# 32-byte gaps between split weights and two groups of split activations in an MLA/GLA decoder trunk

## The chip, the cores and the metric

The kernel runs on one core of a Trainium2 chip. The metric is the device time in microseconds of one execution. Before the change it is 1057.14 us, the median of three runs (1056.98 to 1057.34).

TensorE multiplies: it holds a stationary operand of 128 x 128 and streams a moving operand of up to 512 columns through it; sums collect in PSUM. In the profile a product is a MATMUL on PE with its LDWEIGHTS on PEld. VectorE is DVE, ScalarE is ACT, GpSimd is POOL, and SyncE (SP) starts most transfers. The operands of products lie in SBUF, where a tile takes the same bytes in each of 128 partitions; "at 32 modulo 128" says where in a partition it starts.

## The reference

Two layers, each a mixer and an MLP, all in float32 over a residual stream x of 512 tokens x 1024:

```python
for i in range(DEPTH):                       # 2
    xn = rms_norm(x, norm_mix[i])
    if i % 2 == 0:
        mix = mla_mixer(xn, ...)             # 8 heads, low-rank q and kv, rotary part, causal softmax
    else:
        mix = gla_mixer(xn, ...)             # 4 heads, gated linear attention, gate of rank 16
    x = x + mix
    xn = rms_norm(x, norm_mlp[i])
    x = x + jnp.square(jax.nn.relu(xn @ w_up[i])) @ w_down[i]   # 1024 -> 4096 -> 1024
return rms_norm(x, final_norm)
```

## The kernel before

**Split operands.** A float32 operand is kept as two tiles of the type float32r: `hi`, a rounded copy made on ACT, and `lo`, the rest, made on DVE (`split`, lines 102 to 107). A product is then three products, hi·hi, hi·lo and lo·hi, all into the same PSUM bank (`mm3`, lines 109 to 114). So nearly every product stands in a long row of products of the same shape, each with its own stationary operand.

**Where the operands live.** Four kinds of tile hold most operands:

- `wh` and `wl` hold split weights: three buffers each, filled by `piece` from the raw tiles `wraw` (loaded by SP) or, in the MLPs, `comb`.
- `set_A` holds both parts of one tile of split activations: 8 buffers of 4096 bytes, handed out by `both_parts`. The normalised input X of every mixer and MLP is here (`Norm.scaled`), as are V of the first mixer and the last weights of the second MLP.
- `set_B` holds one part each: 16 buffers of 2048 bytes, handed out by `slot("B")`. The hidden values of the MLPs, the latent values of the first mixer and the heads' outputs are here.
- Pools of their own hold the rest: `cq` and `ckv` (latent q and kv of the first mixer), `T1` to `T4` (combined inputs of the MLP), the tiles of both attentions. The profile leaves numbers out, so it shows both groups as `set` and T1 to T4 as `T`.

The allocator lays tiles out one after another, in the order in which their tags are first asked for, on multiples of 32 bytes. The order of first use is: constants, x, `wraw`, `wh`, `wl`, `set_A`, `set_B`, temporaries (`tmp`, `acc`, `rstd`), small statistics with `rtok`, then the pools that are opened and closed per stage.

**The stages.** The first mixer starts from weights loaded in five parts, each split and followed by the split of the x tiles it meets (the loop at the program's end that fills `w0`). Its input projection (line 408 and lines 112 to 114) has X moving under wh or wl; the projection to V has wh or wl moving and latent tiles stationary; the projections from the latent tiles have cq moving under weights, or weights moving over cq (the rotary part of q); then attention by heads and an output projection with the heads' outputs moving.

Each MLP (`mlp`) works through the 4096 hidden values in blocks of 512, seven of them with a scheme of seven smaller products in place of eight. Its up products (`up_product`, line 939) are 256 columns wide: weights stationary, X (set_A) or T1 to T4 moving, in runs of 24. Its down products (`down_product`, line 948) are 512 wide: hidden values (set_B) stationary, weights moving, in runs of 12. The two kinds alternate. The last block of the first MLP goes through line 1133 (weights stationary, hidden values in set_B moving), that of the second through line 1168 (hidden values stationary, weights split into set_A moving).

The second mixer (`gla`) has input projections of both forms: `proj_qk` with X moving, `b_type` with X stationary and weights moving.

A scheduler orders the instructions of each engine; data dependences and a few written-out orders (`keep_in_program_order`, `issue_after`) bind it.

Of the kernel before, what the change touches and what calls it, by code (L numbers as in the profile page):

```python
# [10 lines left out]
F32 = mybir.dt.float32  # L11
# [7 lines left out]
P = 128  # L19
D = 1024  # L20
S = 512
NT = S // P
# [28 lines left out]
def trunk_kernel(ctx: ExitStack, tc: tile.TileContext, t_in: dict, out: bass.AP):  # L51
# [4 lines left out]
    sb = ctx.enter_context(tc.tile_pool(name="sb", bufs=1))  # L56
    count = [0]

    def uname(s):
        count[0] += 1  # L60
        return f"{s}_{count[0]}"
# [40 lines left out]
    def split(src, hi, lo, hi_eng=ACT, lo_eng=DVE, order=lambda i: i):  # L102
        if hi_eng is ACT:
            order(ACT.activation(hi, src, AF.Copy))  # L104
        else:
            hi_eng.tensor_copy(hi, src)
        lo_eng.tensor_tensor(lo, src, f(hi), ALU.subtract)  # L107
# [29 lines left out]
    def piece(raw, a, n, order=lambda i: i):  # L137
        hi = sb.tile([P, a, n], F32R, tag="wh", bufs=3, name=uname("wh"))
        lo = sb.tile([P, a, n], F32R, tag="wl", bufs=3, name=uname("wl"))
        split(raw, hi, lo, order=order)  # L140
        return hi, lo
# [1055 lines left out]
    def gla(layer, nrm, vtag, ytag):  # L1197
# [82 lines left out]

        own = tmp((P, NT, P))
        DVE.tensor_tensor(own, nrm.rstd.rearrange("p (t c) -> p t c", t=NT), ident.unsqueeze(1).to_broadcast([P, NT, P]), ALU.mult)
        rtok = sb.tile([P, NT], F32, tag="rtok", name="rtok")
        DVE.reduce_sum(rtok, own, AX.X)


# [363 lines left out]
    warm = bank("a")  # L1650
    for _ in range(9):
        PE.matmul(warm[:, :P], ones128, ones128, start=True, stop=True)
    w0 = []
    for k0, k1 in ((0, 1), (1, 2), (2, 4), (4, 6), (6, 8)):
        w = piece(raw0[:, k0:k1], k1 - k0, KL, tc.keep_in_program_order)
        w0 += [(w, i) for i in range(k1 - k0)]
        for j in range(k0, k1):
            nrm.scaled(j, xT[j], tc.keep_in_program_order)
    mla_pools = []
    for name in ("mla_keep", "mla_pre"):  # L1660
        pool_es = ExitStack()
# [25 lines left out]
    mlp(0, n_mlp0, n_mix1)  # L1687
    psum_layout(False)
    Y, begun = gla(0, n_mix1, "B", "B")
    n_mlp1 = Norm(ND, inv_dr, "mlp", ND)  # L1690
    out_proj(t_in["gla_w_o"][0], Y, n_mlp1, begun)
# [23 lines left out]
def build(nc, shapes):  # L1715
    args = {}
    for name, (shape, dt) in shapes.items():
        args[name] = nc.dram_tensor(f"in_{name}_dram", shape, dt, kind="ExternalInput").ap()
    o = nc.dram_tensor("out_0_dram", (S, D), F32, kind="ExternalOutput").ap()
    with tile.TileContext(nc) as tc:  # L1720
        trunk_kernel(tc, args, o)
# [22 lines left out]
```

## Time and profile before

| | |
|---|---|
| median of 3 runs | 1057.14 us |
| profiled execution, its own time | 1057.37 us |
| span, first to last instruction | 1055.6 us |
| mean granted TensorE clock | 0.999 |
| PE busy | 1045.5 us, 99% of the span |
| PEld busy | 913.7 us, 87% |
| DVE busy | 876.0 us, 83% |
| ACT busy | 698.6 us, 66% |
| POOL busy | 113.4 us, 11% |
| mean DMA rate over the span | 142 GB/s |

A row of the groups reads: line, engine, operation, output<-inputs, the array's shape, the output's or moving operand's shape, xcount | busy us in total, mean ns of one | idle time of the engine just before, and what ended it. "ps<-T,wh" is a product into PSUM whose inputs are a T tile and a wh tile. A row of the chain reads: start in us, length in us, engine, output, line, and how many in a row. A row of the timeline reads: start, length, engine, line, operation, operands, shape, count.

### The profile page before, as it was taken

The page shows a single profiled execution, that of the slowest core. Times are in us where ns is not written, and L with a number is a line of the kernel's source. Part 1 is how long each engine was busy: PE and PEld are TensorE (multiplying, and loading weights), DVE is VectorE, ACT ScalarE, POOL GpSimd, SP SyncE. Part 2 cuts the span into 40 slices and gives each one's busy share as a digit, 9 for nine tenths or more (in the row PEclk, how much of TensorE's full clock was granted, in tenths as well). Part 3 has the DMA queues.
Part 4 walks back from the last instruction along what each step waited for, and adds up shares of the span by engine and source line. Part 5 has one row for each costly group of instructions (what it writes and reads, how often), then busy time and mean ns, then how long its engine had stood idle before and what let it go on. Part 6 is the DMA issues. An engine that isn't in the chain of part 4 may idle for free.

```text
span 1055.6 us, 15598 instructions
## 1 busy us (share of the span) xinstructions
PE 1045.5 (99%) x5966; PEld 913.7 (87%) x5966; DVE 876.0 (83%) x1340; ACT 698.6 (66%) x1074; POOL 113.4 (11%) x128
## 2 busy tenths in 40 slices
PE   9999999999999999999999999999999999999997
PEld 7888888889999999998888888878889999999985
DVE  7899977979889889898686498469889989989993
ACT  7667664577777767766445565655667777777784
POOL 7410011201101111000000000000011010010000
PEclk9999999999999999999999999999999999999999
DMA  7311235866966976842322221444496696696622
GB/s 231 90 51 41 81 79 160 238 176 150 235 181 150 229 192 146 221 147 93 90 80 80 80 80 51 126 105 132 110 248 132 178 254 140 176 249 152 165 81 80
DMA packets 120493, 149.97 MB, mean 142 GB/s; under 512 B 9345, under 2 KB 86145, under 8 KB 120289
## 3 DMA queue, kind: packets, MB, share of 16 engines
q1 hardware_dynamic: 95920, 117.76, 34.4%
q0 software_dynamic: 22400, 29.36, 17.4%
q10 hardware_dynamic: 2096, 1.84, 0.6%
q8 instruction: 47, 0.77, 0.3%
q14 instruction: 30, 0.24, 0.1%
HBM read 144.49 MB, written 4.19 MB: 141 GB/s over the span
## 4 chain that ended last, share of the span: by engine, by line
PE 95%; ACT 2%; DVE 2%; issue 0%; DMA 0%; ACTq 0%; SPq 0%; DVEq 0%
PE ps L939 26%; PE ps L948 25%; PE ps L112 10%; PE ps L114 10%; PE ps L113 10%; PE ps L1133 2%; PE ps L1388 2%; PE ps L129 1%; PE ps L1168 1%; PE ps L408 1%; PE ps L1515 1%; DVE wl L107 0%; PE ps L671 0%; PE ps L1438 0%; PE ps L667 0%
## 5 line engine op out<-in xcount | busy, mean ns | idle before, releaser
L948 PE MATMUL ps<-wh,set 128*128 128x512 f32 x784 | 258.5, 390 | 0.0
L107 DVE TENSOR_TENSOR wl<-wraw,wh 128x1024 fp32r<-128x1024 f32 x139 | 169.4, 1221 | 39.7 <-ACT wh L104 39.4
L104 ACT ACTIVATE wh<-wraw 128x1024 fp32r<-128x1024 f32 x139 | 145.9, 1053 | 82.1 <-PE ps L113 38.3
L948 PEld LDWEIGHTS ps<-wh,set 128*128 128x128 f32 x784 | 147.3, 188 | 28.8
L104 ACT ACTIVATE wh<-comb 128x1024 fp32r<-128x1024 f32 x112 | 118.8, 1061 | 62.8 <-PE ps L939 41.9
L939 PE MATMUL ps<-T,wh 128*128 128x256 f32 x896 | 159.8, 279 | 0.0
L948 PE MATMUL ps<-wl,set 128*128 128x512 f32 x392 | 153.7, 392 | 0.0
L107 DVE TENSOR_TENSOR wl<-comb,wh 128x1024 fp32r<-128x1024 f32 x112 | 136.7, 1220 | 18.6 <-ACT wh L104 16.9
L939 PEld LDWEIGHTS ps<-T,wh 128*128 128x128 f32 x896 | 140.5, 188 | 4.5
L939 PE MATMUL ps<-T,wl 128*128 128x256 f32 x448 | 125.1, 279 | 1.0 <-DVE wl L107 1.0
L939 PE MATMUL ps<-set,wh 128*128 128x256 f32 x672 | 122.6, 283 | 0.0
L939 PEld LDWEIGHTS ps<-set,wh 128*128 128x128 f32 x672 | 107.4, 191 | 3.2
L112 PE MATMUL ps<-set,wh 128*128 128x512 f32 x280 | 109.3, 392 | 0.7 <-ACT set L1557 0.3
L113 PE MATMUL ps<-set,wh 128*128 128x512 f32 x280 | 109.4, 391 | 0.0
L114 PE MATMUL ps<-set,wl 128*128 128x512 f32 x280 | 109.0, 390 | 0.0
L939 PE MATMUL ps<-set,wl 128*128 128x256 f32 x336 | 95.2, 283 | 0.0
L939 PEld LDWEIGHTS ps<-T,wl 128*128 128x128 f32 x448 | 84.2, 188 | 1.5 <-DVE wl L107 1.4
L948 PEld LDWEIGHTS ps<-wl,set 128*128 128x128 f32 x392 | 73.8, 188 | 11.6
L928 POOL DMA_DIRECT2D comb<-in_mlp_w_down_dram x28 | 33.6, 1201 | 421.0 <-DMA comb<-in_mlp_w_down_dram 155.5
L939 PEld LDWEIGHTS ps<-set,wl 128*128 128x128 f32 x336 | 64.3, 191 | 0.0
L112 PEld LDWEIGHTS ps<-set,wh 128*128 128x128 f32 x280 | 52.5, 188 | 12.6 <-ACT wh L104 1.0
L114 PEld LDWEIGHTS ps<-set,wl 128*128 128x128 f32 x280 | 52.6, 188 | 11.2 <-DVE wl L107 0.4
(396 smaller groups left out, 2024.2 us busy)
## 6 DMA issues: line engine op xcount, KB each, us to landing
comb<-in_mlp_w_down_dram SPq DMA_DIRECT2D x74, 512.0 KB, 5.0
wraw<-in_mlp_w_up_dram SPq DMA_DIRECT2D x32, 1024.0 KB, 5.8
comb<-in_mlp_w_down_dram POOLq DMA_DIRECT2D x28, 512.0 KB, 7.7
wraw<-in_gla_w_in_dram SPq DMA_DIRECT2D x12, 1024.0 KB, 5.3
comb<-in_mlp_w_up_dram SPq DMA_DIRECT2D x14, 512.0 KB, 3.8
comb<-in_mlp_w_up_dram POOLq DMA_DIRECT2D x14, 512.0 KB, 8.4
wraw<-in_mlp_w_up_dram POOLq DMA_DIRECT2D x14, 512.0 KB, 7.2
wraw<-in_mla_w_o_dram SPq DMA_DIRECT2D x4, 1024.0 KB, 5.0
```

What stands on the lines that cost most here:

```text
L104: order(ACT.activation(hi, src, AF.Copy))
L107: lo_eng.tensor_tensor(lo, src, f(hi), ALU.subtract)
L112: PE.matmul(psum, wh, xh, start=start, stop=False)
L113: PE.matmul(psum, wh, xl, start=False, stop=False)
L114: PE.matmul(psum, wl, xh, start=False, stop=stop)
L129: PE.transpose(psum, src, ident[: src.shape[0], : src.shape[0]])
L408: PE.matmul(p, w[:, i, j * P : (j + 1) * P], x, start=start, stop=stop)
L928: POOL.dma_start(t, q(b, *more), accum_op=ALU.add)
L939: PE.matmul(o, a_, x_, start=start and j == 0 and k == 0 and n == 0, stop=k == KH - 1 and n == 2, skip_group_check=True)
L948: PE.matmul(o, x_, w_, start=start and k == 0 and n == 0, stop=k == 1 and n == 2, skip_group_check=True)
L1133: PE.matmul(p, a, x, start=False, stop=k == 3 and n == 2, skip_group_check=True)
L1388: PE.matmul(p[:, t - t0], k[:, t * P : (t + 1) * P], moving[:, t], start=True, stop=True)
```

## The change

Two tiles of 8 float32 values (32 bytes) that nobody reads or writes are asked for at two places: `gap_a` after the first split of weights, and so behind wh and wl and ahead of set_A; `gap_b` after the first x tiles, and so behind set_A and ahead of set_B. And `rtok`, 16 bytes of use in a slot of 32, is asked for with 64 bytes more.

```diff
@@ in gla @@
-        rtok = sb.tile([P, NT], F32, tag="rtok", name="rtok")
+        rtok = sb.tile([P, NT + 16], F32, tag="rtok", name="rtok")[:, :NT]
         DVE.reduce_sum(rtok, own, AX.X)
@@ at the program's end @@
+    def gap(name, n):
+        sb.tile([P, n], F32, tag=name, bufs=1, name=name)
+
     w0 = []
     for k0, k1 in ((0, 1), (1, 2), (2, 4), (4, 6), (6, 8)):
         w = piece(raw0[:, k0:k1], k1 - k0, KL, tc.keep_in_program_order)
+        if k0 == 0:
+            gap("gap_a", 8)
         w0 += [(w, i) for i in range(k1 - k0)]
         for j in range(k0, k1):
             nrm.scaled(j, xT[j], tc.keep_in_program_order)
+    gap("gap_b", 8)
```

In the two built programs the order of instructions and their waits are the same on every engine. The tiles start here (bytes in a partition, and modulo 128):

| tile | before | after |
|---|---|---|
| wraw, first buffer | 36384, 32 | 36384, 32 |
| wh, first buffer | 52768, 32 | 52768, 32 |
| wl, first buffer | 65056, 32 | 65056, 32 |
| set_A, first buffer | 77344, 32 | 77376, 64 |
| set_B, first buffer | 110112, 32 | 110176, 96 |
| tmp, first buffer | 142880, 32 | 142944, 96 |
| rtok | 163616, 32 | 163680, 96 |
| cq, first | 168576, 0 | 168704, 0 |
| ckv, first | 180928, 64 | 181056, 64 |
| T1 to T4, comb | 64 | 64 |

All buffers of a kind have the same place modulo 128, since their sizes are multiples of 128, and so have the pieces of 128, 256 or 512 values that the products take from them. Behind rtok everything lies 128 bytes farther: 32 and 32 of the gaps, 64 of rtok.

## The prediction

> **What bounds the kernel now.** I read the page's first, second and fourth part, then the groups of instructions with shapes kept apart, then the chain that ended last, and last the timeline of TensorE product by product.
>
> ```profile
> PE 1045.5 (99%) x5966; PEld 913.7 (87%) x5966; DVE 876.0 (83%) x1340; ACT 698.6 (66%) x1074; POOL 113.4 (11%) x128
> ...
> PEclk9999999999999999999999999999999999999999
> ...
> PE 95%; ACT 2%; DVE 2%; issue 0%; DMA 0%; ACTq 0%; SPq 0%; DVEq 0%
> ```
>
> TensorE is busy for 99% of the span at the full granted clock, and 95% of the chain that ended last is its products. So what changes the step from one product to the next goes into the time almost in full, and the other engines have room. [...] Steps are read from start to start, or from the chain, which merges a run of products.
>
> ```profile
> L948 PE MATMUL ps<-wh,set 128*128 128x512 f32 x784 | 258.5, 390 | 0.0
> L939 PE MATMUL ps<-T,wh 128*128 128x256 f32 x896 | 159.8, 279 | 0.0
> L948 PE MATMUL ps<-wl,set 128*128 128x512 f32 x392 | 153.7, 392 | 0.0
> L939 PE MATMUL ps<-T,wl 128*128 128x256 f32 x448 | 125.1, 279 | 1.0 <-DVE wl L107 1.0
> L939 PE MATMUL ps<-set,wh 128*128 128x256 f32 x672 | 122.6, 283 | 0.0
> L939 PE MATMUL ps<-set,wl 128*128 128x256 f32 x336 | 95.2, 283 | 0.0
> ```
>
> L939 (the MLP's up products, 256 columns wide) does the same arithmetic with two kinds of moving tile. With T tiles one product's record is 279 ns, with set tiles 283 ns. Both load their weights from wh or wl. What tells the two apart is the place: wh and wl start at 32 modulo 128 bytes, T at 64, set at 32. The chain shows what that is worth as a step:
>
> ```profile
> 301.46 2.80 PE ps L939 x24
> 304.26 2.75 PE ps L948 x12
> 307.00 2.87 PE ps L939 x24
> 309.88 2.75 PE ps L948 x12
> 312.62 2.80 PE ps L939 x24
> ```
>
> The run at 307.00 has set tiles, those at 301.46 and 312.62 T tiles: 2.87/24 = 119.6 ns a step against 2.80/24 = 116.7 ns. No engine's idle time lies in these runs. So the place of operands does move TensorE's step, and apart operands are quicker here, by 2.9 ns.
>
> While a product streams its moving operand, the stationary operand of the next one is loaded:
>
> ```profile
> 54.22 0.39 PE L114 MATMUL ps<-set,cq2l 128*128 128x512 f32 x1
> ...
> 54.23 0.19 PEld L112 LDWEIGHTS ps<-wh,cq0h 128*128 128x128 f32 x1
> ```
>
> The load begins with the product before it (54.23 beside 54.22). The pair that can meet is therefore this product's moving tile and the next one's stationary tile. I call "distance" the second's start minus the first's, modulo 128 bytes. Now the 512-wide products, of which three runs in the first attention layer have different distances:
>
> ```profile
> 40.54 0.39 PE L112 MATMUL ps<-wh,set 128*128 128x512 f32 x1
> ...
> 43.48 0.39 PE L113 MATMUL ps<-wl,set 128*128 128x512 f32 x1
> ...
> 50.48 0.39 PE L113 MATMUL ps<-wl,cq0h 128*128 128x512 f32 x1
> ...
> 57.97 0.40 PE L112 MATMUL ps<-set,cq2h 128*128 128x512 f32 x1
> ...
> 62.84 0.39 PE L113 MATMUL ps<-cq0l,wh 128*128 128x512 f32 x1
> ...
> 64.71 0.39 PE L112 MATMUL ps<-ckv0h,wh 128*128 128x512 f32 x1
> ...
> 65.88 0.39 PE L114 MATMUL ps<-ckv1h,wl 128*128 128x512 f32 x1
> ```
>
> From 40.54 to 43.48 stand 13 steps at distance 0 (wh 32, set 32): 2.94/13 = 226 ns. From 50.48 to 57.97 stand 32 steps at distance 96 (wh or set at 32, cq at 0): 7.49/32 = 234 ns. From 62.84 to 64.71 stand 8 steps at distance 32 (cq 0, wh 32): 1.87/8 = 233.8 ns. From 64.71 to 65.88 stand 5 steps at distance 96 (ckv 64, wh 32): 1.17/5 = 234 ns. So for 512-wide products the sign is the other way round: equal operands give the short step, apart ones cost 6 to 8 ns more.
>
> A long run of equal ones outside this layer gives the value that most of the kernel has:
>
> ```profile
> 481.66 10.92 PE ps L1133 x48
> ```
>
> 10.92/48 = 227.5 ns; the down products above, 2.75/12 = 229.2 ns, since each run of 12 begins out of step after a 256-wide run.
>
> **The change part by part.** It adds no instruction and moves none: on all five engines the order and the waits of the two programs are the same. It moves set_A tiles (32 to 64 modulo 128), set_B tiles and the temporaries behind them (32 to 96); wh and wl stay at 32, and all that lies behind rtok moves by 128 bytes, so T, cq, ckv and the attention tiles keep their place. I counted in the program, product by product, how distances change; four groups matter.
>
> 1. *256-wide, distance 0 to 96*: 970 of them, the set products of L939, 42 runs of 24. Afterwards set_A is at 64 and wh at 32, which is just what T has now. Each run goes from 2.87 to 2.80 us: 42 x 0.07 = -2.9 us.
> 2. *512-wide, 0 to 96*: 531, set_A moving (64) under wh or wl (32): the input projections of both mixers and the MLPs' first block. The same two places as ckv under wh: 234 ns. From 227.5: 531 x 6.5 = +3.5 us. Another ckv run of that layer reads:
>
> ```profile
> 60.77 0.39 PE L112 MATMUL ps<-ckv0h,wh 128*128 128x512 f32 x1
> ...
> 61.93 0.40 PE L114 MATMUL ps<-ckv1h,wl 128*128 128x512 f32 x1
> ```
>
>    5 steps in 1.16 us, 232 ns. I take 233: +2.9 us, with 2.4 and 3.5 as ends.
> 3. *512-wide, 0 to 32*: 452, weights moving (32) with set_A stationary (64), and the last layer's output products. At 233.8 ns for 227.5: +2.8 us. The pair has not these very places in the trace, only their distance.
> 4. *512-wide, 0 to 64*: 1602, the largest group: 1077 of the 1176 products of L948 (wh or wl at 32 moving, set_B at 96 stationary), and 525 others, mostly the output projections with set_B moving. No steady 512-wide run at this distance is in the trace. Bounds: the slowest row, 234 ns, gives 1077 x 4.8 + 525 x 6.5 = +8.6 us; a gain like the 256-wide one, 2.9 ns each, gives -4.6 us. I take 233, near the first end, because both neighbours on either side of 0 (32 and 96) are slow at this width, and 64 lies farther from 0 than either: 1077 x 3.8 + 525 x 5.5 = +7.0 us.
>
> Everything else costs nothing by its rows. Vector and scalar engine also read and write at the moved places, but theirs does not depend on it:
>
> ```profile
> L107 DVE TENSOR_TENSOR wl<-wraw,wh 128x1024 fp32r<-128x1024 f32 x139 | 169.4, 1221 | 39.7 <-ACT wh L104 39.4
> L104 ACT ACTIVATE wh<-wraw 128x1024 fp32r<-128x1024 f32 x139 | 145.9, 1053 | 82.1 <-PE ps L113 38.3
> L104 ACT ACTIVATE wh<-comb 128x1024 fp32r<-128x1024 f32 x112 | 118.8, 1061 | 62.8 <-PE ps L939 41.9
> L107 DVE TENSOR_TENSOR wl<-comb,wh 128x1024 fp32r<-128x1024 f32 x112 | 136.7, 1220 | 18.6 <-ACT wh L104 16.9
> ```
>
> wraw is at 32, comb at 64, wh and wl at 32: 1221 against 1220 ns on DVE, 1053 against 1061 on ACT. Even 8 ns on each of ACT's thousand instructions would be 8 us of an engine that is idle a third of the time; what hides it is ACT's own slack (82.1 us before one of these groups), and TensorE's step, which grows. The few transposes and attention products that change distance (some 60 of 512 columns, a few 256- and 384-wide) may win or lose 0.3 us together.
>
> Sum: -2.9 + 2.9 + 2.8 + 7.0 = +9.8 us. The profiled execution took 1057.4 us (span 1055.6), 0.2 above the median of 1057.14, which is well inside what I claim. Forecast 1067.2 us.
>
> [...]
>
> **The rivals.**
> - *Distance 64 behaves as 0 at width 512.* It would if what repeats had a period of 64 bytes. Then group 4 is 0 and the time 1057.4 + 2.8 = 1060.2 us. Against it: 32 and 96 are alike at width 512, but no row tells 64 from 0 there.
> - *Distance 64 gains at width 512*, as 96 does at 256: 1057.4 + 2.8 - 4.6 = 1055.6 us.
> - *The other side: the 234 ns belong to the attention layer, not to distance.* There TensorE works beside many short ACT and DVE instructions. If those stretch its steps, groups 2 to 4 are 0 and only the gain of group 1 is left: 1054.5 us; if the wide products then gain 2.9 ns as well (2585 x 2.9 = 7.5), 1047.0. It decides where 512-wide products of the input projections, which have long equal runs now, show a step of 227 or less afterwards. Against it: the run at 40.54 lies in the same layer, 10 us earlier, and holds 226 ns.
> - *Nothing happens*, because what I read as distance is something else that T and cq tiles share: 1057.4 us. The places I used for group 1 are the very ones that T has now, which speaks against it.
>
> **How the numbers follow.** Forecast as summed, with group 4 slow: 0.58, 1063.5 to 1071. Distance 64 as 0: 0.20, about 1060. Distance 64 gains: 0.08. The attention layer's rows mislead: 0.10. Nothing: 0.04. The predicted time is 1067.2. The range leaves out the fourth case and the top of the first: 1055.5 (group 4 at its lower end) to 1070.5 (group 4 at 234 ns gives 1068.8, and 1.7 for runs of 12 that never come into step). A change of 0.2%, 2.1 us, is about the least that a measurement of this kernel can tell. Slower by more: 0.58 + 0.20 less a little = 0.77. Faster by more: the fourth case, 0.11 with a little of the third. Within: 0.12.
>
> **What would show it.** Right: L939 runs of 24 with set tiles at 2.80 us and their records at 279 to 280 ns; L948 runs of 12 at about 2.80 instead of 2.75 us; steps of 233 in the output projection (L1133, 11.2 us for 48); PE's busy time up by about 10 us with no new wait. Wrong: L948 at or under 2.75 us (then distance 64 is not slow), or the input projections still at 227 (then the attention layer's rows misled me), or a stall of TensorE that ends with ACT or DVE.

## The result, and the profile after

The changed kernel takes 1066.4 us (median of 3 runs, 1066.1 to 1066.66) against 1057.14 us before: a ratio of 1.0087, 95% interval 1.0064 to 1.011. The forecast was 1067.2 us. The span of the profiled execution grows from 1055.6 to 1064.6 us.

The page of the changed kernel, first, second and fourth part:

```profile
PE 1055.0 (99%) x5966; PEld 913.0 (86%) x5966; DVE 876.8 (82%) x1340; ACT 698.8 (66%) x1074; POOL 112.5 (11%) x128
...
PEclk9999999999999999999999999999999999999999
...
PE 97%; DVE 1%; ACT 1%; issue 0%; DVEq 0%
```

TensorE is busy 9.5 us longer over the same 5966 products, at the same granted clock (0.999); the busy times of the other engines move by less than 1 us. So the loss is in the steps of products. The groups of products, shapes kept apart (line, tiles, shape, count, then busy time and mean ns of one):

```profile
L948 PE MATMUL ps<-wh,set 128*128 128x512 f32 x784 | 262.1, 395 | 0.0
L939 PE MATMUL ps<-T,wh 128*128 128x256 f32 x896 | 161.4, 281 | 0.0
L948 PE MATMUL ps<-wl,set 128*128 128x512 f32 x392 | 154.6, 394 | 0.0
L939 PE MATMUL ps<-T,wl 128*128 128x256 f32 x448 | 125.9, 281 | 1.2 <-DVE wl L107 1.2
L939 PE MATMUL ps<-set,wh 128*128 128x256 f32 x672 | 119.9, 280 | 0.0
L939 PE MATMUL ps<-set,wl 128*128 128x256 f32 x336 | 94.0, 280 | 0.0
```

Against before, the down products (L948) go from 390 and 392 to 395 and 394 ns, the up products with set tiles (L939) from 283 to 280. The T rows go from 279 to 281 ns, and the prediction had left those alone. The chain that ended last, in the first MLP, says the same in steps:

```profile
303.23 2.85 PE ps L939 x24
306.08 2.80 PE ps L948 x12
308.88 2.81 PE ps L939 x24
311.68 2.79 PE ps L948 x12
314.47 2.82 PE ps L939 x24
...
484.71 11.00 PE ps L1133 x48
```

Runs of 12 down products take 2.79 to 2.80 us, where they took 2.75. Of the runs of 24, those with set tiles are at about 2.81 (2.87 before), and those with T tiles (303.23 and 314.47) take 2.85 and 2.82 (2.80 before). The output projection of the last block (L1133) takes 11.00 us instead of 10.92. And the projection to V that stood at 226 ns a step at 40.54 before (weights moving, set_B stationary), on the timeline:

```profile
40.17 0.39 PE L113 MATMUL ps<-wl,set 128*128 128x512 f32 x1
...
43.66 0.40 PE L113 MATMUL ps<-wl,set 128*128 128x512 f32 x1
```

15 steps in 3.49 us, 232.7 ns. The input projection of the first mixer (X in set_A moving, weights stationary), the same 59 steps before and after:

```profile
19.80 0.39 PE L112 MATMUL ps<-set,wh 128*128 128x512 f32 x1
...
33.17 0.39 PE L114 MATMUL ps<-set,wl 128*128 128x512 f32 x1
```

```profile
19.39 0.40 PE L112 MATMUL ps<-set,wh 128*128 128x512 f32 x1
...
33.16 0.39 PE L114 MATMUL ps<-set,wl 128*128 128x512 f32 x1
```

13.37/59 = 226.6 ns before, 13.77/59 = 233.4 ns after.

From the starts of all products in the two traces, the mean per run of products or per step:

| products | before | after | difference |
|---|---|---|---|
| L939, set tiles, 41 whole runs of 24 | 2.872 us | 2.807 us | -2.7 us |
| L939, T tiles, 54 whole runs of 24 | 2.802 us | 2.833 us | +1.6 us |
| L948, 41 runs of 12 after set tiles | 2.747 us | 2.787 us | +1.6 us |
| L948, 55 runs of 12 after T tiles | 2.744 us | 2.801 us | +3.1 us |
| set_A moving under weights, 512 wide, 514 steps | 227.2 ns | 233.1 ns | +3.0 us |
| set_B moving under weights, 455 steps | 227.2 ns | 230.0 ns | +1.3 us |
| weights moving over set_A, 326 steps | 228.5 ns | 232.9 ns | +1.4 us |
| set tiles over set tiles, 93 steps | 227.9 ns | 233.3 ns | +0.5 us |

The sum is +9.8 us, for 9.0 us of span. The difference is in the waits. With the products of the two traces set side by side in their order, the 5863 steps that stay under 250 ns in both grow by 10.2 us together, and the 102 longer ones, most of which hold a wait, shrink by 1.2 us. Of that, 0.4 us is one step, the one from the last warm-up product to the first product of the model (778 to 338 ns).

### The profile page after: what moved, and what is told of

It is laid out like the page before. It is cut to its first block, busy times and chain, and to the rows that moved or that the text cites. A ratio compares the mean times of both kernels' runs of the same rounds, so it can differ in the third digit from the quotient of the medians.

```text
span 1064.6 us, 15598 instructions
## 1 busy us (share of the span) xinstructions
PE 1055.0 (99%) x5966; PEld 913.0 (86%) x5966; DVE 876.8 (82%) x1340; ACT 698.8 (66%) x1074; POOL 112.5 (11%) x128
## 4 chain that ended last, share of the span: by engine, by line
PE 97%; DVE 1%; ACT 1%; issue 0%; DVEq 0%
PE ps L948 26%; PE ps L939 25%; PE ps L112 11%; PE ps L114 11%; PE ps L113 11%; PE ps L1168 2%; PE ps L1133 2%; PE ps L1388 2%; PE ps L129 1%; PE ps L408 1%; PE ps L1515 1%; PE ps L1652 0%; PE ps L671 0%; PE ps L1438 0%; PE ps L667 0%; PE ps L670 0%
## 5 line engine op out<-in xcount | busy, mean ns | idle before, releaser
L948 PE MATMUL ps<-wh,set 128*128 128x512 f32 x784 | 262.1, 395 | 0.0
L948 PEld LDWEIGHTS ps<-wh,set 128*128 128x128 f32 x784 | 147.1, 188 | 30.6
L939 PE MATMUL ps<-T,wh 128*128 128x256 f32 x896 | 161.4, 281 | 0.0
L948 PE MATMUL ps<-wl,set 128*128 128x512 f32 x392 | 154.6, 394 | 0.0
L939 PEld LDWEIGHTS ps<-T,wh 128*128 128x128 f32 x896 | 141.1, 188 | 5.2
L939 PE MATMUL ps<-T,wl 128*128 128x256 f32 x448 | 125.9, 281 | 1.2 <-DVE wl L107 1.2
L939 PE MATMUL ps<-set,wh 128*128 128x256 f32 x672 | 119.9, 280 | 0.0
L112 PE MATMUL ps<-set,wh 128*128 128x512 f32 x280 | 110.6, 396 | 0.6 <-ACT set L1557 0.3
L113 PE MATMUL ps<-set,wh 128*128 128x512 f32 x280 | 110.9, 397 | 0.0
L114 PE MATMUL ps<-set,wl 128*128 128x512 f32 x280 | 110.1, 394 | 0.0
L939 PEld LDWEIGHTS ps<-set,wh 128*128 128x128 f32 x672 | 105.3, 188 | 3.8
L939 PE MATMUL ps<-set,wl 128*128 128x256 f32 x336 | 94.0, 280 | 0.0
L939 PEld LDWEIGHTS ps<-T,wl 128*128 128x128 f32 x448 | 84.4, 188 | 1.7 <-DVE wl L107 1.6
L948 PEld LDWEIGHTS ps<-wl,set 128*128 128x128 f32 x392 | 73.6, 188 | 13.5
L114 PEld LDWEIGHTS ps<-set,wl 128*128 128x128 f32 x280 | 52.6, 188 | 12.5 <-DVE wl L107 0.4
L939 PEld LDWEIGHTS ps<-set,wl 128*128 128x128 f32 x336 | 63.2, 188 | 0.0
```

Source lines behind the costliest of these rows:

```text
L112: PE.matmul(psum, wh, xh, start=start, stop=False)
L113: PE.matmul(psum, wh, xl, start=False, stop=False)
L114: PE.matmul(psum, wl, xh, start=False, stop=stop)
L939: PE.matmul(o, a_, x_, start=start and j == 0 and k == 0 and n == 0, stop=k == KH - 1 and n == 2, skip_group_check=True)
L948: PE.matmul(o, x_, w_, start=start and k == 0 and n == 0, stop=k == 1 and n == 2, skip_group_check=True)
```

## The experiments

The theory on record: the step depends on the width and on the distance (next stationary start minus moving start) modulo 128 bytes. Rivals: modulo something longer; no effect of distance at all, with other engines stretching the steps.

**Products alone.** No other engine works beside the rows, the operands are fixed, and only where the stationary slices start is changed: first 48 products 512 wide per distance (L82 to L91: 0, 16, 32 and so on), then 48 that are 256 wide (L92 to L101).

```python
for i in R: order(PE.matmul(o(i, 512), w(i, 0), m(i, 512), start=True, stop=True))   # R = range(48)
for i in R: order(PE.matmul(o(i, 512), w(i, 4), m(i, 512), start=True, stop=True))   # 4 floats = 16 bytes on
...
```

> This kernel leaves the model out: it runs only rows of 48 products, each row with one distance between the moving tile and the next stationary tile, DVE and ACT idle, and writes two sums as output. Distance theory: the step depends on the distance and the width alone. 512 wide: 226.7 ns (10.9 us a row) at distance 0 and 128, 233 to 234 ns (11.2 us) at 32, 64 and 96. 256 wide: 120 ns (5.76 us) at 0 and 128, 116.7 to 118 ns (5.60 to 5.66 us) at 32, 64 and 96; nothing is known of 16, 48, 80 and 112. Rival, other engines: without DVE and ACT beside it every row of one width has the same step, about 227 and 117 to 120 ns. [...]

The page's busy line, and four rows of the chain (distances 0, 64 and 128 at width 512; 64 at width 256):

```profile
PE 235.6 (92%) x1288; PEld 203.6 (80%) x1288; DVE 1.3 (1%) x2; ACT 4.6 (2%) x3; POOL 0.2 (0%) x4
```

```profile
24.41 10.88 PE b L82 x48
...
68.57 11.19 PE b L86 x48
...
113.32 11.20 PE b L90 x48
...
158.26 5.44 PE b L96 x48
```

10.88/48 = 226.7 ns at distance 0, 11.19/48 = 233.1 at 64, with DVE and ACT idle. So the place of the stationary operand alone moves the step, and the rival that blamed the attention layer's short instructions is out. Two misses: at width 512, 128 is as slow as 64 (233.3), though modulo 128 it is 0; and 256-wide products at 64 take 5.44/48 = 113.3 ns, less than the mean step of any run of up products in the model.

**One part of the change at a time, first form.** Only set_A moved by 32 bytes, with set_B and all behind it 128 bytes on:

```diff
+        if k0 == 0:
+            gap("gap_a", 8)
...
+    gap("gap_b", 24)
```

> Only the 256-wide set products, the input projections and the last layer's products change distance; the down products of the MLP stay at 0. Distance theory: -2.8 (42 runs of 24 from 2.87 to 2.80 us) +3 (X moving, 96) +2.3 (weights moving or the last products, 32 and 96) = +2.5 us, about 1059.7; L948 runs of 12 stay at 2.75 us. Rival, the shift of everything behind by 128 bytes disturbs the T products as in the changed kernel (+1.6 us): about 1061.3, T records at 281 ns. Rival, only group 1 counts: 1054.4.

Measured: 1068.16 us, ratio 1.0099 (1.0082 to 1.0116), over 8 us above the expectation. Only set_B moved by 64 bytes, with all behind rtok 128 bytes on:

```diff
-        rtok = sb.tile([P, NT], F32, tag="rtok", name="rtok")
+        rtok = sb.tile([P, NT + 16], F32, tag="rtok", name="rtok")[:, :NT]
...
+    gap("gap_b", 16)
```

> Only set_B moves, to 96 modulo 128: 1077 down products and some 520 output projection products go from distance 0 to 64, set_A stays at 32. Distance theory: 1077 x 4 ns + 520 x 4 ns = +6.4 us, about 1063.5; L948 runs of 12 at 2.80 us, L939 set runs at 2.87, T runs at 2.80. Rival, T disturbed by the shift of 128 bytes: +8, T records at 281 ns. Rival, distance 64 is as 0 when set_A keeps its place: 1057.1.

Measured: 1066.88 us, 1.0091 (1.0076 to 1.0106), 3 us above. And only what lies behind rtok, 128 bytes on:

```diff
+        rtok = sb.tile([P, NT + 32], F32, tag="rtok", name="rtok")[:, :NT]
```

> Only what lies behind rtok moves, by 128 bytes: no distance changes modulo 128. Distance theory with a period of 128 bytes: 1057.1, nothing changes, T records stay at 279 ns and T runs at 2.80 us. Rival, the period is longer (256 bytes or more): T runs at 2.81 to 2.85 us, +1.6 us, 1058.7, as in the changed kernel.

Measured: 1059.3 us, 1.0021 (1.0011 to 1.003). By distance modulo 128 nothing changed in it. Its chain:

```profile
301.64 2.85 PE ps L939 x24
304.50 2.73 PE ps L948 x12
307.22 2.87 PE ps L939 x24
```

Runs with T tiles go from 2.80 to 2.85 us, the down products behind them from 2.75 to 2.73, the runs with set tiles stay at 2.87. So a move by 128 bytes changes the step: the period is longer than 128, and the change's own 128 bytes behind rtok cost time.

**The period.** Products alone again, distances 0 to 496 by 16 bytes, then 512, 576 and 1024 (512 wide: L82 onwards; 256 wide: L117 onwards).

> This kernel leaves the model out too: rows of 48 products at distances of 0 to 496 bytes in steps of 16, then 512, 576 and 1024, 512 and then 256 columns wide. Theory of a long period (512 bytes, the step between two stationary pieces of one tile): the rows at 512 and 1024 are as that at 0 (10.9 us at width 512, 5.75 at 256), the row at 576 is as that at 64 (11.2 and 5.44), and 256 is not as 0. Rival, a period of 256 bytes: the row at 256 is as that at 0 and the second half repeats the first. Rival, only nearness counts (the same bytes or the same line, no period): 512 and 1024 are slow at width 512, 11.2 us.

Rows of the chain, 512 wide at 0, 64, 128 and 256:

```profile
24.67 10.88 PE b L82 x48
...
68.82 11.19 PE b L86 x48
...
113.58 11.20 PE b L90 x48
...
202.50 10.88 PE b L98 x48
```

256 wide at 0, 64, 192 and 576:

```profile
413.31 5.75 PE b L117 x48
...
436.07 5.44 PE b L121 x48
...
481.55 5.44 PE b L129 x48
...
600.35 5.66 PE b L150 x48
```

In ns per step (length over 48):

| distance modulo 256 | 0 | 32 | 64 | 96 | 128 | 160 | 192 | 224 |
|---|---|---|---|---|---|---|---|---|
| 512 wide | 226.7 | 233.1 | 233.1 | 234.2 | 233.3 | 233.1 | 229.0 | 233.3 |
| 256 wide | 119.8 | 118.3 | 113.3 | 118.8 | 118.5 | 120.0 | 113.3 | 116.7 |

The rows at 256 to 496 take what the rows 256 bytes ahead of them take, to 0.01 us in 10.88 to 11.24 (512 wide) and in 5.44 to 5.76 (256 wide). So the step of these rows has a period of 256 bytes; the rival of 512 falls. One row of the scan breaks it: 576, which is 64 modulo 256, takes 5.66 us and not 5.44. The first run of products alone has another such row: at 192, 256 wide, it took 5.65 us, where the scan has 5.44 at the same distance. The rows ahead of the slow ones were at 512 and at 128, those ahead of the quick ones at 48 and at 176. So a row of 48 too can stay at the slower step (117.7 and 117.9 ns against 113.3), and distance does not settle it alone.

Read modulo 256, the places of the kernel before are: set under or over weights 0; T under weights 224 (T at 64, weights at 32), 116.7 ns, which is the 2.80 us of its runs; cq and ckv 96 or 160, 233 to 234 ns. After: T at 192, so 96 (118.8 ns); set_A moving 224 (233.3 or 116.7); weights moving over set_A 32 (233.1) and over set_B 64 (233.1); set_B moving 192 (229.0). This also accounts for the misses of the first three parts: all of them moved T to distance 96, and the set_A part moved set_B to distance 128, where by the starts of the products the runs of 12 of L948 took 2.79 us in place of 2.75 (+4.0 us in all). The products with set_B moving (L1133 among them, 232.4 ns for 227.1) went there as well.

All tiles behind wl moved by 512 bytes is the counter-test in the model:

```diff
+        if k0 == 0:
+            gap("gap_a", 128)
```

> set_A, set_B and all behind them move by 512 bytes, wh and wl stay: every distance between them changes by 512. Theory of a period of 512 bytes: nothing changes, 1057.1, L948 runs of 12 at 2.75 us, L939 at 2.87 (set) and 2.80 (T). Rival, a period above 512, or nearness alone: L948 at 2.79 to 2.80 and the input projections at 233 ns, 1066 or more, as with 128 bytes for set_B.

Measured: 1057.18 us, ratio 1.0 (0.999 to 1.001). Moving tiles by this much costs nothing that was measured.

**One part at a time, by 256 bytes.** The set_A part, with everything behind it moved by a multiple of 256:

```diff
+        if k0 == 0:
+            gap("gap_a", 8)
...
+    gap("gap_b", 56)
```

> The set_A part of the change alone: set_A 32 bytes on, all that lies behind it 256 bytes on. If the step follows width and distance modulo 256, T, cq, ckv and set_B keep their steps: T runs of 24 at 2.80 us (records 279 ns), L948 runs of 12 at 2.75, L1133 10.9 for 48; L939 set runs go to 2.80; the input projections to 233 ns. Sum: -2.9 + 2.9 + 2.8 = +2.8, 1060 us. If it follows it modulo 512 or more, T records go to 281 again and the time is 1062 us or above.

Measured: 1058.83 us, 1.0018 (1.0009 to 1.0028). T and L948 keep their runs, set tiles have T's 2.80, in a row:

```profile
296.67 2.80 PE ps L939 x24
299.47 2.75 PE ps L948 x12
302.21 2.80 PE ps L939 x24
```

Rows of products alone moved the stationary operand; here it is the moving one of L939 that goes 32 bytes on, which makes the distance 224, and its runs take what that distance gives (24 x 116.7 ns = 2.80 us). So it is the difference of the two places that counts.

The rise of 0.18%, 1.9 us, is 0.9 us less than expected: the 326 steps of weights over set_A had 228.5 ns before and not 227.5, so they lose less.

The set_B part:

```diff
+        rtok = sb.tile([P, NT + 48], F32, tag="rtok", name="rtok")[:, :NT]
...
+    gap("gap_b", 16)
```

> The set_B part alone: set_B 64 bytes on, all behind it 256 bytes on, set_A where it was. Modulo 256: L948 runs go from 2.75 to 2.80 us (1077 x 3.8 ns = +4.1), products with set_B moving to 229 ns (525 x 1.5 = +0.8), T stays at 2.80, L939 set at 2.87: +4.9, 1062 us. With the set_A part alone and the run in which only the tiles behind rtok moved (+2.2) the three should add up to what the whole change cost, +9 us. If a longer period counts, T records go to 281 ns here too and the time is 1064 us or above.

Measured: 1064.48 us, 1.0071 (1.0054 to 1.0087), 2.5 us above the expectation. Its chain has T at 2.80, set tiles at 2.87 and the down products at 2.79 to 2.83:

```profile
306.26 2.79 PE ps L948 x12
309.04 2.87 PE ps L939 x24
311.92 2.80 PE ps L948 x12
314.72 2.81 PE ps L939 x24
317.52 2.83 PE ps L948 x12
```

The 96 runs of L948 average 2.806 us, 0.061 more than before: +5.8 us instead of the +4.1 expected. So the group that the set_B gap touches is most of the loss. The three parts apart (1.0018, 1.0071 and 1.0021) multiply to 1.0110, the upper end of the whole change's interval, 1.0087 being measured. By the intervals the two are not told apart. In the traces, about half of the excess is in the T runs, which average 2.854 us with the tiles behind rtok moved alone and 2.833 us in the whole change: T lies at distance 96 in both, so a run's length depends also on the runs beside it (as the 2.73 above).

**Can the 113.3 ns be had?** Before, with T alone moved by 32 bytes to distance 192:

```diff
         fast = es.enter_context(tc.tile_pool(name=f"fast{layer}", bufs=1, reuse_waits="tile"))
+        fast.tile([P, 8], F32, tag="lead", name="lead")
```

> The kernel before with one change: 32 bytes ahead of T1 in the MLP's pool, so that T lies at distance 192 instead of 224 from wh and wl. If the rows of 48 hold in this kernel's runs of 24, T runs go from 2.80 to 2.72 us (113.3 ns), 1344 x 3.4 = -4.5 us: 1052.6 us. If the short step at 192 needs a row that begins in step (a row at distance 576, the same modulo 128 and 256, did not reach it), T runs stay at 2.80 to 2.83 and the time is 1057 to 1058.5 us.

Measured: 1059.15 us, 1.002 (1.0011 to 1.003). The same with set_A moved as well, by 64 bytes (gap_a 16 floats, gap_b 48):

> The same, and set_A 64 bytes on with all behind it 256 bytes on: X also at distance 192 under weights of 256-wide products. If rows of 48 hold: L939 set runs from 2.87 to 2.72 (1006 x 6.3 ns = -6.3), T -4.5, products of 512 with X moving 229 ns (+0.8), weights moving over X at distance 64, 233 ns (+2.5): -7.5, 1049.6 us. If the step of 113.3 is not reached in runs of 24 (both at about 118): T +1.6, set -1.6, and +3.3: 1060.4 us. If ACT or DVE become the bound of the MLP before that, idle time of PE ahead of L939 that ends with wh or wl grows above the 1.0 us of before.

Measured: 1060.69 us, 1.0035 (1.0022 to 1.0048). In both it came out as in the second branch, the first of them 0.7 us above it. T runs of the first of the two (L940 and L949 here are L939 and L948, one line lower):

```profile
312.27 2.83 PE ps L940 x24
315.10 2.76 PE ps L949 x12
```

2.83/24 = 117.9 ns: the short step is not reached. Why, the next run asked: products alone, in the MLP's form.

```python
for r in range(4):
    for i in range(24): order(PE.matmul(o(i, 256), w(i, d), m(i, 256), start=True, stop=True))
    for i in range(12): order(PE.matmul(o(i, 512), w(i, e), m(i, 512), start=True, stop=True))
```

> The model is left out: only products, in the MLP's form: 24 of 256 columns at one distance, then 12 of 512 at another, four times, for distances 0, 32, 64, 96, 192, 224, 320 and 576 of the first by 0, 64 and 192 of the second. If the 113.3 ns of long rows at 64 and 192 hold in runs that follow other products, runs of 24 take 2.72 us there and the two kernels with T at 192 were slow for a reason outside the places. If a run has to begin in step, 24 products at 64, 192, 320 and 576 take 2.80 to 2.85 us as in those kernels (117.9 ns), those at 224 2.80 and at 0 2.87. Runs of 12 take 2.75 us at 0, 2.80 at 64 and 2.76 at 192.

Its chain, one pair each for distances 0 and 0 (L83, L84); 192 and 0 (L95, L96); 224 and 0 (L98, L99); 64 and 64 (L113, L114); 192 and 64 (L119, L120):

```profile
27.50 2.75 PE b L84 x12
30.25 2.87 PE b L83 x24
...
114.20 2.82 PE b L95 x24
117.02 2.73 PE b L96 x12
...
136.42 2.80 PE b L98 x24
139.22 2.75 PE b L99 x12
...
248.35 2.73 PE b L113 x24
251.07 2.79 PE b L114 x12
...
292.88 2.83 PE b L119 x24
295.70 2.80 PE b L120 x12
```

Most runs of the model come out here without the model: 2.87 and 2.75, 2.80 and 2.75, 2.82 instead of the 2.83 of T at 192. T at 96 does so only as a pair: 2.82 and 2.77 us at distances 96 and 0, where the model with the tiles behind rtok moved had 2.85 and 2.73 (5.59 against 5.58 us). Whether a run of 24 at distance 64 or 192 gets 113.3 ns depended on the run ahead of it: not behind products at 0 (2.83 us at 64, 2.82 at 192), yes at 64 behind products at 64 (2.73), and no at 192 behind products at 64 (2.83). Behind 512-wide products at distance 192 both got it (2.731 us at 64, 2.720 at 192, by the starts of the products; these rows are not shown). That pair of 2.72 and 2.75 us would be 5.47 us, against 5.62 and 5.55 in the kernel before. A whole kernel at those places was not run: L948, the input and output projections and the MLP share tiles, and what its other products would lose is open.

**The opposite on a small scale.** Before, with cq and ckv moved to distance 0:

```diff
+            if j == 0:
+                keep.tile([P, 40], F32, tag="pad_q", name="pad_q")
             hi, lo = (keep.tile([P, S], F32R, tag=f"cq{j}{x}", name=f"cq{j}{x}") for x in "hl")
...
+                    if j == 0:
+                        keep.tile([P, 48], F32, tag="pad_kv", name="pad_kv")
                     hi, lo = (keep.tile([P, S], F32R, tag=f"ckv{j}{x}", name=f"ckv{j}{x}") for x in "hl")
...
+                keep.tile([P, 40], F32, tag="pad_end", name="pad_end")
```

> The kernel before with pads inside the first mixer's pool, so that cq and ckv start at 32 modulo 256 like the weights and all behind them lies 512 bytes farther. The change's opposite on a small scale: some 150 products of 512 columns go from distance 96 or 160 to 0, from 233 to 234 ns to 226.7. By distance -1.0 us, 1056.1 us, and the steps from L113 cq onwards read 227. If the attention layer's 234 ns came from other engines, nothing changes.

Measured: 1056.69 us, ratio 0.9993 (0.9984 to 1.0002): in time not told apart from before. The timeline of the products under cq tells more:

```profile
51.19 0.40 PE L113 MATMUL ps<-wl,cq0h 128*128 128x512 f32 x1
...
53.05 0.39 PE L112 MATMUL ps<-wh,cq0h 128*128 128x512 f32 x1
...
58.04 0.39 PE L113 MATMUL ps<-wl,cq1h 128*128 128x512 f32 x1
```

From 53.05 to 58.04 stand 22 steps, 226.8 ns each; at the old places these products took 234. But the 8 steps from 51.19 to 53.05, with transposes (L129) shortly ahead of them, take 232.5. The runs of L948 before begin like that too: behind the up products their first five steps average 231.8 ns, the other seven 226.7. The 141 such steps under 250 ns average 229.5 ns, for 233.5 before: -0.6 us.

## Why the prediction came out as it did

- *TensorE's step takes the whole change; nothing else moves.* Right: PE's busy time +9.5 us for a span of +9.0, and no new wait; the waits shrink by 1.2 us.
- *Group 1, set tiles of L939, -2.9 us.* Right: 2.872 to 2.807 us a run, -2.7. Modulo 256 too the places are those that T had, 224.
- *Group 2, set_A moving at width 512, +2.9.* Right in size: 233.1 ns, +3.0. The distance it was priced by was misread: set_A is at 224 modulo 256, ckv at 96. That both are slow is luck.
- *Group 3, weights moving over set_A, +2.8.* Right in sign, too large: 228.5 to 232.9 ns for 326 steps and 227.9 to 233.3 for 93, +1.9. The row it was priced by is at 160 modulo 256 and these products are at 32; that both take 233.1 ns is luck again.
- *Group 4, distance 64 at width 512, taken at 233 ns, +7.0.* Right for the wide rows of L948: 233.1 ns in products alone, and +4.7 us for 4.1. Wrong for those with set_B moving: modulo 256 these are at 192, 230.0 ns, +1.3 us instead of 2.9, and L1133 at 11.00 us and not 11.2.
- *"T, cq, ckv and the attention tiles keep their place"* is the step that failed. It rests on the period of 128 bytes, which no row of before could tell from 256. T moved by 128 bytes, from 224 to 96, and its 54 whole runs lost 1.6 us. That the forecast still came out within 0.8 us of the time is luck, errors of opposite sign: the T runs (+1.6) and L948 (0.6 above its term) against the set_B products (-1.6), group 3 (-0.9) and the waits that shrank.
- *The rivals.* Distance 64 as 0, or gaining, at width 512: out, by L948 at 2.80 us. The attention layer instead of distance: out, by the input projection, whose step went from 226.6 to 233.4 ns, and by products alone with DVE and ACT idle. Nothing happens: out, by a ratio of 1.0087 (1.0064 to 1.011). No effect of the place at all: out too, by rows of products alone with 226.7 and 233.1 ns, in which nothing but the place of the stationary operand differs.

What the runs show is that the step follows width and distance (226.7 ns at 512 columns and 119.8 at 256, both at distance 0; 233.1 at 512 columns and 64) and the row ahead (2.83 and 2.73 us for 24 products at 64). That this product's moving tile and the next one's stationary tile are a pair that can meet was my guess; no run shows a meeting. Nor do these rows tell whether the next product's stationary operand counts or the product's own, since within a row both lie at the same distance modulo 256.

## What to carry to other kernels

In this kernel, which TensorE bounds, the place of operands was worth 0.9% of the time (1066.4 us against 1057.14). In one like it, look at the same instruction in rows that differ only in tiles, and read its step from start to start, not from its record (L948 before: records of 390 ns, steps of 229). A move by 512 bytes cost nothing here (1057.18 us) and one by 128 bytes did (1059.3), so pad by whole periods where places shall be kept, and measure the period before trusting it. Short runs that alternate need not get the step of a long row (117.9 ns in T's runs of 24 at distance 192, 113.3 in a row of 48), so price them from runs of their own length behind their own neighbours.

## What the runs showed of the hardware that was not expected

- The step of float32r products repeated in the scan with a period of 256 bytes in the distance (one row, 576, excepted), with the sign depending on width: at 512 columns 0 was the shortest (226.7 ns; 240 and 16 are within 0.4 ns of it), at 256 columns 64 and 192 were (113.3 against 119.8 at 0).
- In some rows nearly every product takes the same step: before, 226 to 227 ns in the 59 steps of the input projection (512 columns, distance 0) and, from the second step on, 116 to 117 in the T runs of L939 (256 columns, 224). In others the steps go up and down: after, 230 to 236 ns in the same 59 steps (distance 224) and 114 to 123 in the T runs (96). Why was not found.
- The same distance modulo 256 gave two steps behind different rows: 113.3 ns at 64 and 117.9 at 576 in one scan, 113.3 at 192 in that scan and 117.7 in the run before it, 2.72 and 2.83 us for 24 products at 192 in the alternating runs.
